# One visit instead of two: the products of scores and values behind the last chunk of a head pair

## The chip, the cores and the metric

The kernel runs on one core of a Trainium2 chip. The metric is the device time of one execution in microseconds (us); the median of three runs of the kernel before is 1099.41 us (1097.35 to 1099.85).

## The reference

One decoder layer on a sequence of 512 tokens with 2048 channels in float32. The normalised input is projected; one half of the result goes through a recurrent mixer with 16 heads of 64 channels, the other through a pooling group; both are gated, joined, projected back and added to the input, and a gated per-layer embedding and a last normalisation follow. What matters here is the recurrence of a head and the group normalisation behind it:

```python
    def step(S, inp):
        r_t, w_t, k_t, v_t, kk_t, a_t = inp
        sa = jnp.einsum('bhvk,bhk->bhv', S, -kk_t)
        S = (S * w_t[:, :, None, :]
             + sa[..., None] * (kk_t * a_t)[:, :, None, :]
             + v_t[..., None] * k_t[:, :, None, :])
        y_t = jnp.einsum('bhvk,bhk->bhv', S, r_t)
        return S, y_t
...
        y = wkv7_scan(rh, wh, kh, vh, kk, ah)
        y = head_group_norm(y, ln_w[i], ln_b[i])
```

## The kernel before, in words

**Chunks, hops and pairs.** The 16 heads are taken as 8 pairs (j, 128 channels each), and the 512 tokens as 8 chunks (ch) of 64 tokens. Within a chunk the recurrence is written with matrices, so that only the state goes from chunk to chunk. The function recur (from L756) does this for one pair. For each chunk it issues on TensorE:

- the output product (L784, py<-sbd,ar): the state (sbd) times the chunk's queries and keys. VectorE adds one half of it to mv (L787, zs);
- the solve product (L793, psu; pu in the profile), whose result ScalarE copies into uv (L797), the chunk's corrected values;
- the state product (L802, pss; ps in the profile), from which VectorE makes the next state (L809, sbd), and GpSimd the part s0p that the hop behind it adds (L816).

Each of these three steps hangs on the one before through VectorE or ScalarE. The way from one to the next is called a hop. So that TensorE does not wait, pump(n) puts n matmuls of other work behind each: 9 behind the state product (HC3), 6 behind the output product (HC1), 9 behind the solve product (HC2). This other work is one long stream: the large projections of coming pairs and of the pooling group (zk, zr, zv, zg, zb in the profile, 128x512 each, with weights and inputs split into a high and a low part, three matmuls per block) and at the end the embedding's (pple).

**The outputs.** The outputs of four chunks share one PSUM bank: a tile py of 128x512, one for chunks 0 to 3 and one for chunks 4 to 7. To the output products are added the products of scores (mt) and values (uv) within a chunk (L824): for each of four chunks and each of the two heads a 128x64 by 128x64 product into 64 of the bank's 128 partitions. TensorE is used there as two tiles of 64 columns, and an even chunk's and an odd chunk's product alternate. In the profile they are py<-uv,mt, 128*64; a visit is an unbroken run of them. One visit stands behind the state product of chunk 3, the other behind chunk 7's solve product, since the last chunk needs no new state. Behind each visit ScalarE copies the two halves of the bank into ysb (L830).

**Behind the hops.** From ysb VectorE makes statistics (L845, eight), aggregates (L847, eight), the inverse root (L850, then L143 to L151) and the normalised values (L854, eight). The function finish transposes them on TensorE (L861, pyt), and ScalarE and VectorE apply scale, bonus and gate.

**Between two pairs** the function gather (from L678) prepares the next one: on TensorE the decay and rate products (pu, pa), transposes of values (pv) and keys (pbk), the products pmv and the key norm's pss (L566), with pump between them; on ScalarE the tanh (L532, sig), the exponentials (L539 pw, L540 ipw) and copies (L690, L700 bkn, L712, L713); on VectorE the running sum of the log decay (L533, L534, sig).

**PSUM.** Four pools share the eight banks. The pool psY has two banks, and in turn they hold half of the score tiles (pm, in chunk 0), py of chunks 0 to 3, py of chunks 4 to 7 and pv of the next pair. The pool psM has three, for most other products, pbk, pmv and pss among them.

**What sets the order.** Matmuls are held in the order of the program (mm, L157 in the profile). On the other engines the framework's planner puts the instructions in order: by the program's order as priority, by its own estimate of when inputs are there, and with the hop's own steps (L787, L797, L809) far ahead by a high_priority. Each engine then works through its list in that order. The weights of the stream come by DMA from SyncE's queue; ScalarE rounds them (L132, whi) and VectorE takes the rest (L133, wlo).

## Time and profile before

| | |
|---|---|
| runs, us | 1099.85, 1097.35, 1099.41 |
| span of the profiled execution, us | 1095.9 |
| all py<-uv,mt records | 256, 16 visits of 16, 222 ns each (median) |
| ysb<-py copies on ScalarE | 32, 367 ns each |
| statistics st<-ysb on VectorE | 64, 214 ns each |
| aggregates mvr<-st on VectorE | 64, 152 ns each |

The profiled execution is one of its own; the table gives its span, from the first to the last instruction, and the times of the runs include what lies around it. The matmul records of this profile come two for each product of plain float32, which is done in two passes. Ends of matmuls are modelled and overlap; the distance from one start to the next is what a matmul costs in a stream. A row of the timeline has the start and length in us, the engine (PE is TensorE, PEld its weight loads, DVE VectorE, ACT ScalarE, POOL GpSimd), the line, the operation, output<-inputs, shapes and the count of merged records; in brackets stands the idle time before it and what ended it. A row of the waits has who waited, for whom, total us, times and longest.

### The profile page before, as it was taken

To read this page: it belongs to the slowest core of one execution; us is meant where nothing else is said; L and a number is where in the kernel's file an instruction comes from. 1 tells how busy PE (TensorE), PEld (TensorE's weight loads), DVE (VectorE), ACT (ScalarE), POOL (GpSimd) and SP (SyncE) were. 2 spreads that over 40 slices of the span, in tenths; PEclk is the share of its full clock that TensorE was granted. 3 is DMA by queue.
4 is the path that set the end of the run, shared out by engine and by line. 5 is a ranking of instruction groups with operands and counts; after the bars stand their busy time and mean duration, and the time that the engine had idled before them with its cause. 6 is when DMAs were issued, how large, how long until landed. Compare 5 with 4: busy or idle time off the path is not lost.

```text
span 1095.9 us, 17196 instructions
## 1 busy us (share of the span) xinstructions
PE 1070.8 (98%) x6060; PEld 877.6 (80%) x6060; DVE 708.2 (65%) x1835; ACT 448.3 (41%) x917; POOL 76.9 (7%) x180
## 2 busy tenths in 40 slices
PE   5999999999999999999999999999999999999996
PEld 4888878887788888788878788888888888888885
DVE  6687867878688679678886956454433424445366
ACT  7633535345335335353343344543222222233337
POOL 2100110110110110100101101000000000000000
PEclk9999999999999999999999999999999999999999
DMA  7433433332423333333334242775534438455534
GB/s 233 116 96 97 111 92 84 96 100 73 120 82 105 104 92 89 96 82 93 91 94 119 79 138 93 232 233 169 172 124 136 167 99 244 137 189 137 181 106 154
DMA packets 178486, 138.56 MB, mean 126 GB/s; under 512 B 34678, under 2 KB 139743, under 8 KB 178399
## 3 DMA queue, kind: packets, MB, share of 16 engines
q1 hardware_dynamic: 157694, 103.89, 32.1%
q10 hardware_dynamic: 20704, 33.56, 9.8%
q8 instruction: 48, 0.79, 0.3%
q14 instruction: 40, 0.32, 0.1%
HBM read 118.02 MB, written 18.87 MB: 125 GB/s over the span
## 4 chain that ended last, share of the span: by engine, by line
PE 86%; DVE 5%; DMA 4%; ACT 3%; issue 1%; SPq 0%; ACTq 0%; DVEq 0%
PE acc_o L157 16%; PE zb L157 14%; PE acc_g L157 14%; PE zv L157 8%; PE zk L157 7%; PE zg L157 7%; PE zr L157 7%; PE py L157 2%; PE pple L157 2%; PE pm L157 1%; PE pu L157 1%; DMA n<-nd 1%; PE pp L157 1%; DMA raw_g<-in_w_pg_dram 1%; PE ps L157 1%
## 5 line engine op out<-in xcount | busy, mean ns | idle before, releaser
L133 DVE TENSOR_TENSOR wlo_g<-raw_g,whi_g 128x512 fp32r<-128x512 f32 x84 | 57.0, 685 | 79.6 <-ACT whi_g L132 76.5
L157 PE MATMUL zb<-hhi,whi_b 128*128 128x512 f32 x256 | 107.0, 418 | 0.0
L133 DVE TENSOR_TENSOR wlo_o<-raw_o,whi_o 128x512 fp32r<-128x512 f32 x64 | 43.9, 690 | 91.4 <-ACT whi_o L132 91.4
L157 PE MATMUL zb<-hhi,wlo_b 128*128 128x512 f32 x256 | 100.5, 393 | 0.0
L157 PE MATMUL acc_o<-whi_o,ylo 128*128 128x512 f32 x256 | 100.2, 391 | 0.0
L157 PE MATMUL acc_o<-whi_o,yhi 128*128 128x512 f32 x256 | 99.9, 390 | 0.0
L157 PE MATMUL zb<-hlo,whi_b 128*128 128x512 f32 x256 | 99.9, 390 | 0.0
L157 PE MATMUL acc_o<-wlo_o,yhi 128*128 128x512 f32 x256 | 99.8, 390 | 0.0
L132 ACT CAST whi_g<-raw_g 128x512 fp32r<-128x512 f32 x84 | 51.9, 620 | 102.7 <-PE acc_g L157 55.4
L157 PE MATMUL acc_g<-whi_g,x2hi 128*128 128x512 f32 x208 | 81.3, 391 | 0.0
L157 PE MATMUL acc_g<-wlo_g,x2hi 128*128 128x512 f32 x208 | 80.9, 389 | 0.0
L157 PE MATMUL acc_g<-whi_g,x2lo 128*128 128x512 f32 x208 | 80.7, 389 | 0.0
L132 ACT CAST whi_o<-raw_o 128x512 fp32r<-128x512 f32 x64 | 39.9, 623 | 97.0 <-PE acc_o L157 96.7
L816 POOL TENSOR_SCALAR s0p<-sbd,pw 64x64 f32<-64x64 f32 x96 | 56.6, 589 | 322.8 <-DVE sbd L809 255.0
L132 ACT CAST whi_b<-raw_b 128x512 fp32r<-128x512 f32 x64 | 39.7, 621 | 86.5 <-PE zv L157 35.4
L133 DVE TENSOR_TENSOR wlo_b<-raw_b,whi_b 128x512 fp32r<-128x512 f32 x64 | 43.8, 685 | 34.2 <-ACT whi_b L132 32.9
L157 PEld LDWEIGHTS zb<-hhi,wlo_b 128*128 128x128 f32 x256 | 48.0, 188 | 11.1
L661 DVE TENSOR_TENSOR xw<-xw,tm 128x60 f32<-128x60 f32 (+24 forms) x248 | 52.1, 210 | 6.8
L157 PEld LDWEIGHTS acc_o<-wlo_o,yhi 128*128 128x128 f32 x256 | 48.1, 188 | 10.3 <-DVE wlo_o L133 0.4
L157 PEld LDWEIGHTS acc_o<-whi_o,yhi 128*128 128x128 f32 x256 | 48.1, 188 | 9.7
L157 PEld LDWEIGHTS acc_o<-whi_o,ylo 128*128 128x128 f32 x256 | 48.1, 188 | 9.8
L157 PEld LDWEIGHTS zb<-hhi,whi_b 128*128 128x128 f32 x256 | 48.2, 188 | 8.5
(285 smaller groups left out, 2550.0 us busy)
## 6 DMA issues: line engine op xcount, KB each, us to landing
raw_b<-in_w_in_dram SPq DMA_DIRECT2D x64, 256.0 KB
raw_o<-in_w_out_dram SPq DMA_DIRECT2D x64, 256.0 KB
raw_g<-in_w_pg_dram SPq DMA_DIRECT2D x64, 256.0 KB
raw_k<-in_w_in_dram SPq DMA_DIRECT2D x32, 256.0 KB
raw_r<-in_w_in_dram SPq DMA_DIRECT2D x32, 256.0 KB
raw_v<-in_w_in_dram SPq DMA_DIRECT2D x32, 256.0 KB
raw_g<-in_w_in_dram SPq DMA_DIRECT2D x32, 256.0 KB
n<-nd SPq DMA_DIRECT2D x16, 256.0 KB
```

The costliest lines, as they stand in the source:

```text
L132: nc.scalar.copy(hi, raw)
L133: nc.vector.tensor_tensor(lo, raw, hi.bitcast(F32), ALU.subtract)
L157: i = nc.tensor.matmul(*a, **k)
L661: nc.vector.tensor_tensor(xw[:, 0:n_, s + 1:32], xw[:, 0:n_, s + 1:32], tm[:, 0:n_, 0:w_], ALU.add)
L816: nc.gpsimd.tensor_scalar(s0p[hc, :], nxt[hc, hc], pcn[hc], None, ALU.mult)
```

## The change

The visit behind chunk 3 is taken out, and its eight products and two copies are put in front of those behind chunk 7. Both py tiles are kept in a dictionary until then. Order and number of the products, the copies and everything else of the program stay.

```diff
@@ -770,7 +770,7 @@
         ysb = rw.tile([P, NT, P], F32, name=f"ysb{j}", tag="t", bufs=4)
-        py = None
+        pys = {}
         for ch in range(NCH):
@@ -778,7 +778,8 @@
             if ch % 4 == 0:
-                py = psY.tile([P, T], F32, name=f"py{j}_{ch}", tag="y")
+                pys[ch // 4] = psY.tile([P, T], F32, name=f"py{j}_{ch}", tag="y")
+            py = pys[ch // 4]
             zs = zsp[par]
@@ -814,20 +815,21 @@
-            if ch % 4 == 3:
-                for qq in range(2):
-                    for h in range(2):
-                        for pr in range(2):
-                            c_ = ch - 3 + 2 * qq + pr
-                            yr = slice(64 * pr, 64 * pr + 64)
-                            o_ = (2 * qq + pr) * P + 64 * h
-                            mm(py[yr, o_:o_ + 64], mt[:, pr, 2 * (c_ // 2) + h, pr, :],
-                                             uv[:, c_, 64 * h:64 * h + 64], start=False, stop=True,
-                                             skip_group_check=True)
-                py4 = py.rearrange("p (s c) -> p s c", c=P)
-                for pr in range(2):
-                    yr = slice(64 * pr, 64 * pr + 64)
-                    nc.scalar.copy(ysb[yr, q - 1:q + 1, :], py4[yr, pr::2, :])
+            if ch == NCH - 1:
+                for c0 in range(0, NCH, 4):
+                    py = pys[c0 // 4]
+                    for qq in range(2):
+                        for h in range(2):
+                            for pr in range(2):
+                                c_ = c0 + 2 * qq + pr
+                                yr = slice(64 * pr, 64 * pr + 64)
+                                o_ = (2 * qq + pr) * P + 64 * h
+                                mm(py[yr, o_:o_ + 64], mt[:, pr, 2 * (c_ // 2) + h, pr, :],
+                                   uv[:, c_, 64 * h:64 * h + 64], start=False, stop=True, skip_group_check=True)
+                    py4 = py.rearrange("p (s c) -> p s c", c=P)
+                    for pr in range(2):
+                        yr = slice(64 * pr, 64 * pr + 64)
+                        nc.scalar.copy(ysb[yr, c0 // 2:c0 // 2 + 2, :], py4[yr, pr::2, :])
             step()
```

## The prediction

> **What bounds the kernel now.** I read the page first, then the waits of TensorE, then the timeline around the two places where the products of scores and values stand.

> ```profile
> span 1095.9 us, 17196 instructions
> PE 1070.8 (98%) x6060; PEld 877.6 (80%) x6060; DVE 708.2 (65%) x1835; ACT 448.3 (41%) x917; POOL 76.9 (7%) x180
> PE 86%; DVE 5%; DMA 4%; ACT 3%; issue 1%; SPq 0%; ACTq 0%; DVEq 0%
> 137.90:720.00 582.10, 578.60 (x3658) 470.94 (x3658) 442.17 (x1330) 245.79 (x535) 64.23 (x112) 1.00 0.37 104
> ```

> The last row is a stretch that holds all eight pairs' hops (its columns: length, then busy time of PE, PEld, DVE, ACT, POOL, then the granted clock, 1.00, and DMA). TensorE is busy 578.6 of 582.1 us there, so a change counts by what it does to TensorE's stream: work taken out of it, or a wait put into it. The waits in the same stretch (total, times, longest) are few:

> ```profile
> PE py L157 <- DVE sbd L809: 1.6, 4, 0.9
> PE pss L157 <- ACT bkn L700: 0.9, 2, 0.5
> PE pu L157 <- DVE zs L787: 0.4, 1, 0.4
> PEld py L157 <- DVE sbd L809: 5.2, 9, 1.4
> ```

> The profiled execution is known by its span, 1095.9 us; the median of the three runs, 1099.41, lies 3.5 us above it and includes what surrounds the program. I work out differences on the span and put them on the median. 0.2%, about what a measurement of this kernel can tell from no change, is 2.2 us.

> **The visit that goes (behind chunk 3).** Pair 0, TensorE, behind chunk 3 and then, for comparison, behind chunk 5, where no products stand:

> ```profile
> 155.36 0.38 PE L157 MATMUL ps<-uv,bkn 128*128 128x128 f32 x2
> 155.68 0.69 PE L157 MATMUL py<-uv,mt 128*64 128x64 f32 x16
> 156.29 0.50 PE L157 MATMUL zk<-hhi,whi_k 128*128 128x512 f32 x1
> 158.47 0.38 PE L157 MATMUL py<-sbd,ar 128*128 128x128 f32 x2
> ...
> 162.38 0.38 PE L157 MATMUL ps<-uv,bkn 128*128 128x128 f32 x2
> 162.52 0.47 PE L157 MATMUL zr<-hhi,whi_r 128*128 128x512 f32 x1
> 164.68 0.38 PE L157 MATMUL py<-sbd,ar 128*128 128x128 f32 x2
> ...
> 605.95 0.38 PE L157 MATMUL ps<-uv,bkn 128*128 128x128 f32 x2
> 609.06 0.38 PE L157 MATMUL py<-sbd,ar 128*128 128x128 f32 x2
> ```

> Between the state product and the next chunk's output product lie nine matmuls of the projection in both cases. With the visit that takes 158.47 - 155.36 = 3.11 us, without it 164.68 - 162.38 = 2.30. Pair 6, the last two rows, gives 3.11 again; the other pairs lie between. The visit costs 0.81 us, 8 x 0.81 = 6.5 us in all, and all of it lies on TensorE's path. (Eight products are sixteen records: each is done in two passes.)

> **The visit that grows (behind chunk 7).** The sixteen records reappear there, behind sixteen others. A visit with 32 small tiled records exists in the kernel already, pmv in the gathering step:

> ```profile
> 564.57 1.15 PE L157 MATMUL pmv<-uv,mt 64*64 64x64 f32 x32
> 565.65 0.50 PE L157 MATMUL pss<-kqh,blk 128*128 128x512 f32 x1
> 181.12 0.69 PE L157 MATMUL py<-uv,mt 128*64 128x64 f32 x16
> 208.26 2.06 PE L157 MATMUL pm<-ar,bk 64*128 64x128 f32 x32
> ```

> 32 records take 1.15 us where 16 take 0.69: 16 more cost 0.46 us. The next large matmul starts 565.65 - 564.57 = 1.08 after the visit's first record, against 156.29 - 155.68 = 0.61 for 16, which is 0.47. So the streaming part moves and the rest, 0.81 - 0.47 = 0.34 us, vanishes: getting into and out of the products is paid once per pair and not twice. New is that the merged visit goes from one PSUM bank to another in its middle. The scores (pm, last row) change the bank at every product and run 32 records of twice the columns in 2.06 us, about twice 1.15 less the fixed part, so I take 0 for the change of bank; the upper end is a whole visit's fixed 0.34 us, at which nothing would be gained. 8 x 0.34 gives **-2.7 us**.

> **The cover that chunk 3's hop loses.** Its state product now has 2.30 us until the next output product, as at the other hops. The wait of that output product is VectorE's sbd. The tightest case behind chunk 3 is one of the pairs where a weight split stands between the two updates:

> ```profile
> 306.73 0.29 DVE L809 SCALAR_TENSOR_TENSOR sbd<-ps,pw,s0p 64x64 f32<-64x64 f32 x1
> 308.44 0.38 PE L157 MATMUL py<-sbd,ar 128*128 128x128 f32 x2
> ```

> The update ends at 307.02, 1.42 us before its reader. 0.81 less leaves 0.61 us, so I put the lost cover at nothing; what it costs if VectorE comes late is the second rival.

> **The copies, and what is queued behind them.** ScalarE's two copies of the first four chunks and VectorE's four statistics and four aggregates leave the hop of chunk 3, where nobody on TensorE waited for them, and join the others behind chunk 7. Pair 0 there:

> ```profile
> 181.88 0.74 ACT L830 COPY ysb<-py 64x256 f32<-64x256 f32 x2 [0.27 <-PE py L157]
> 184.36 0.30 ACT L524 CAST us<-ur 128x128 fp32r<-128x128 f32 x1 [1.73 <-PE pu L157]
> 187.58 0.63 ACT L539 ACTIVATE pw<-sig 128x512 f32<-128x512 f32 x1 [0.57 <-DVE rs L151]
> 189.27 1.07 ACT L700 COPY bkn<-pbk 128x512 f32<-128x512 f32 x2
> 182.66 0.61 DVE L845 BATCH_NORM_STATS2 st<-ysb 128x6 f32<-128x64 f32 x4 [0.32 <-ACT ysb L830]
> 183.18 0.37 DVE L847 BATCH_NORM_AGGREGATE mvr<-st 128x2 f32<-128x6 f32 x4
> 183.58 0.17 DVE L850 TENSOR_SCALAR ve<-mvr 128x8 f32<-128x8 f32 x1
> 186.26 1.22 DVE L534 TENSOR_TENSOR_SCAN sig<-seg,sig 128x512 f32<-128x512 f32 x1
> 189.64 0.75 DVE L854 TENSOR_SCALAR ysb<-ysb,mvr,rs 128x64 f32<-128x64 f32 x3
> 184.84 0.60 PE L161 MATMUL pv<-ident,sv 128*128 128x128 f32 x4
> 189.90 0.50 PE L157 MATMUL pss<-kqh,blk 128*128 128x512 f32 x1 [0.45 <-ACT bkn L700]
> 193.22 0.60 PE L161 MATMUL pyt<-ident,ysb 128*128 128x128 f32 x4
> ```

> ScalarE is idle 1.73 us behind its copies, so 0.74 us more of them fits, and what is queued behind them (the casts of us and then sig) still finds its input late. The first bank is now held until the end of the pair, and the transposes pv want one of the two banks of its pool; the first two copies end about 1.5 us behind the visit's start, the transposes come 184.84 - 181.12 = 3.7 us behind it: no wait. VectorE's chain gets later: the last copy ends 0.74 later, so four of the statistics start at about 2.3 us behind the visit's start; four statistics (0.52 from the first to what follows) and the aggregates (0.1 each with what follows, two of them in the gap ahead of the last copy) put L850 at about 3.4 where it stands 183.58 - 181.12 = 2.46 now. That is 0.9 later, or 0.44 against TensorE, whose own stream is 0.46 later there. For the normalised outputs that is covered: L854 ends at 190.39, its reader pyt stands at 193.22. The tightest is the last pair, where 712.67 - 711.79 = 0.88 us are left for the 0.44:

> ```profile
> 711.03 0.76 DVE L854 TENSOR_SCALAR ysb<-ysb,mvr,rs 128x64 f32<-128x64 f32 x3
> 712.67 0.60 PE L161 MATMUL pyt<-ident,ysb 128*128 128x128 f32 x4
> ```

> Nothing that moves issues a DMA or stands in the queues of SyncE and GpSimd.

> The place with no slack is the other wait of the list above: VectorE's scan (L534) shares its queue with this chain, ScalarE's pw waits for the scan, the bkn copies stand behind pw, and TensorE's pss waits 0.45 us for a bank that a bkn copy frees. The scan is threaded between the steps of the chain as soon as its input is there, so with the chain shifted it can take a place one or two steps earlier and start when it starts now. I take 0, with bounds of -0.9 (both listed waits of pss vanish) and +0.44 in each of the three pairs (0, 2 and 4) where pw stands ahead of bkn, +1.3 us.

> [...] By the rows, the copy reads 181.88 - 181.81 = 0.07 us behind the end of 16 records, and behind 32 records it is no later:

> ```profile
> 565.76 0.26 ACT L712 COPY zs<-pmv 64x128 f32<-64x128 f32 x1 [1.16 <-PE pmv L157]
> ```

> Those 32 end at 564.57 + 1.15 = 565.72, 0.04 us before the copy of an idle ScalarE. [...]

> The sum is -2.7 us: 1099.4 - 2.7 = **1096.7 us**.

> **The rivals.**

> Pss waits longer (no measurable change). If the scan keeps its place in VectorE's order, three gathers lose 0.44 us: -2.7 + 1.3 = -1.4, or 1098.0. For it speaks that the order is written by a planner that has its own idea of the durations; against it, that in pairs 1, 3 and 5 the bkn copies already stand ahead of pw. [...] I give it 2 in 100, as the row above shows no tail.

> The planner turns pw and bkn round (more gain). With the scan planned later, the bkn copies are ready first and pss waits for nothing, as in pairs 1, 3 and 5: -2.7 - 0.9 = -3.6, or 1095.8.

> The hop of chunk 3 loses its cover (slower). The mechanism: in the stretch that shrinks from 3.11 to 2.30 us, a weight split (0.69 us) or two stand ahead of the state update on VectorE, as at nine other places now, where the weight load waits 5.2 us in all. With the longest wait that TensorE shows there, 0.9 us, in each pair, the time is -2.7 + 8 x 0.9 = +4.5, or 1103.9. It eats the gain from 0.34 us per pair on and is slower by over 0.2% from 0.34 + 0.28 = 0.62 on. Against it: 0.61 us of slack are left at the tightest pair, and the statistics leave that very stretch.

> The change does not do what it says: the matmuls keep the order of the program, so the visits do merge; that only a move within an idle stretch results is excluded by 578.6 of 582.1.

> **How the numbers follow.** The sum as it stands 50 in 100, more gain 12, longer waits of pss 26 (the tail among them), merged visit with a price at the change of bank 4, the lost cover 8. The likeliest case by itself spans 1096.2 to 1097.3, half a microsecond for waits that fall elsewhere in a new order. The range goes from the case with more gain, with 1 us of spread of the runs below it, 1094.8, to the longer waits of pss with 1.4 above, 1099.4. Faster by over 0.2% (below 1097.2) are the case with more gain and nine tenths of the likeliest: 0.57. Within 0.2%: the rest of the likeliest, the pss case and the bank: 0.35. Slower: 0.08.

> **What would show it.** Right: one visit of 32 py records per pair, about 1.15 us long, with the next large matmul about 1.08 behind its start; 2.30 us from state product to output product behind chunk 3; the sum of the hops shorter by 0.34 us per pair. Wrong: a gap inside the 32 records, waits of py for sbd behind chunk 3, or waits of pss for bkn above 0.9 us in all.

## The result and the profile after

The changed kernel takes 1105.41 us (median of six runs, 1102.93 to 1110.24) where the kernel before, run beside it, takes 1099.56 (six runs, 1097.35 to 1100.93). The ratio is 1.0061, with a 95% interval of 1.0043 to 1.0080: it is slower by 5.9 us, where 2.7 us less were predicted. In the experiments further down, one of the eleven runs of the kernel before with its preparation held back took 2747 us, for no cause that the record shows, and the ratios leave it out.

The page of the changed kernel opens with its span and the engines' busy time:

```profile
span 1103.6 us, 17200 instructions
PE 1072.4 (97%) x6060; PEld 878.1 (80%) x6060; DVE 708.0 (64%) x1835; ACT 449.6 (41%) x917; POOL 76.4 (7%) x180
```

The span is 7.7 us longer than before, TensorE's busy time 1.6 us, so most of the loss is waiting (the visits alone should have made that busy time shorter; a stretch at half clock, below, makes it longer). The waits of TensorE in the changed kernel (who, for whom, total us, times, longest) name the places:

```profile
PE py L157 <- DVE sbd L810: 2.8, 4, 1.0
PE pyt L161 <- DVE ysb L856: 2.8, 4, 1.3
PE pq L157 <- DVE y L734: 2.4, 2, 1.6
...
PE pss L157 <- ACT bkn L700: 0.7, 2, 0.4
```

The waits of pyt (the transposes of the normalised outputs, in finish) and of pq (what hangs on VectorE's L734, in the same step) were not in the list before. The four transposes of a group wait one by one for their pieces, and most of that is put down to their weight loads:

```profile
PEld pyt L161 <- DVE ysb L856: 5.0, 14, 0.8
```
TensorE's timeline in pair 0 shows that the visits themselves did what was predicted, first chunk 3, then chunk 7:

```profile
156.16 0.38 PE L157 MATMUL ps<-uv,bkn 128*128 128x128 f32 x2
...
158.46 0.38 PE L157 MATMUL py<-sbd,ar 128*128 128x128 f32 x2
181.11 1.15 PE L157 MATMUL py<-uv,mt 128*64 128x64 f32 x32
182.19 0.50 PE L157 MATMUL zv<-hhi,whi_v 128*128 128x512 f32 x1
```

From state product to output product behind chunk 3 it is 158.46 - 156.16 = 2.30 us; the 32 records take 1.15 us without a gap, and the next large matmul starts 1.08 us behind the first. Taking every matmul of the two profiles in order and comparing when it starts, the eight visits behind chunk 3 give 0.80 us each and the eight behind chunk 7 cost 0.47 each: -2.6 us. The same comparison gives the loss: +6.6 at pyt, +2.5 at pq, +0.9 at py for sbd, +1.6 in a stretch at half clock. That is +9.0, of the 9.6 us by which the stretch of the pairs gets longer. Behind the pairs 1.6 us come off: from the last transpose on, the profiled execution of before takes 382.7 us, the changed kernel 381.1, and so do most other kernels here, so that part says nothing about the change.

**Where pyt waits.** A word on the pairs first: in the gathering step behind pair 1, the products pv, pbk and pmv are pair 2's, but pu, pss and VectorE's preparation (kp, ar, bk and what they need) are already pair 3's; the same holds behind every pair. "The preparation" and "the prepared pair" mean that one here. VectorE's timeline in this step, before:

```profile
258.11 0.17 DVE L850 TENSOR_SCALAR ve<-mvr 128x8 f32<-128x8 f32 x1
258.32 0.17 DVE L143 TENSOR_SCALAR rs<-ve 128x8 int32<-128x8 int32 x1
...
263.40 0.16 DVE L151 SCALAR_TENSOR_TENSOR rs<-nt,rs 128x8 f32<-128x8 f32 x1
263.48 0.42 DVE L593 TENSOR_SCALAR tha<-tha 128x512 f32<-128x512 f32 x1
263.81 1.88 DVE L854 TENSOR_SCALAR ysb<-ysb,mvr,rs 128x64 f32<-128x64 f32 x8
```

And after:

```profile
260.10 0.17 DVE L852 TENSOR_SCALAR ve<-mvr 128x8 f32<-128x8 f32 x1
260.20 0.69 DVE L133 TENSOR_TENSOR wlo_b<-raw_b,whi_b 128x512 fp32r<-128x512 f32 x1
260.81 0.17 DVE L143 TENSOR_SCALAR rs<-ve 128x8 int32<-128x8 int32 x1
...
264.88 0.69 DVE L594 TENSOR_TENSOR ar<-sr,pw 128x512 f32<-128x512 f32 x1
265.48 0.16 DVE L151 SCALAR_TENSOR_TENSOR rs<-nt,rs 128x8 f32<-128x8 f32 x1
265.56 0.68 DVE L596 TENSOR_TENSOR bk<-kp,ipw 128x512 f32<-128x512 f32 x1
266.16 0.16 DVE L149 TENSOR_TENSOR nt<-rs,ve 128x8 f32<-128x8 f32 x1
266.24 0.75 DVE L597 SCALAR_TENSOR_TENSOR ar<-sk,dprm,pw 128x512 f32<-128x512 f32 x1
266.90 0.16 DVE L150 TENSOR_TENSOR nt<-nt,rs 128x8 f32<-128x8 f32 x1
266.98 0.69 DVE L568 TENSOR_SCALAR kk<-pss 128x512 f32<-128x512 f32 x1
...
268.35 1.82 DVE L856 TENSOR_SCALAR ysb<-ysb,mvr,rs 128x64 f32<-128x64 f32 x8
```

The chain of the normalised outputs (ve, eleven small steps of the inverse root, eight normalised pieces) takes 263.81 + 1.88 - 258.11 = 7.6 us before and 268.35 + 1.82 - 260.10 = 10.1 after. No step of it got slower: more of the preparation (L594, L596, L597) and of other work that is ready (L568, L734, a weight split L133) stands between its steps, 0.4 to 0.75 us each. Before, such work stood between the steps too, but fewer pieces of it. To compare kernels I set each time against the start of the step's first large product (pu<-uhh,us), and take the transposes with it. Before and after on TensorE:

```profile
258.46 0.39 PE L157 MATMUL pu<-uhh,us 128*128 128x512 f32 x1
267.49 0.60 PE L161 MATMUL pyt<-ident,ysb 128*128 128x128 f32 x4
```

```profile
259.52 0.39 PE L157 MATMUL pu<-uhh,us 128*128 128x512 f32 x1
268.98 1.57 PE L161 MATMUL pyt<-ident,ysb 128*128 128x128 f32 x4 [0.26 <-DVE ysb L856]
```

Before, the chain starts 0.35 us ahead of pu, ends 7.23 behind it, and pyt starts at 9.03. After, it starts 0.58 behind pu, ends at 10.65, and the four transposes take 1.57 us instead of 0.60, each waiting for its piece. So a start that is 0.92 us later became an end that is 3.4 later.

**Why the start is 0.92 later and not the predicted 0.44.** Of the two lists of answers about kql (the low part of the prepared pair's split keys), before and after, these lines give its first and last start:

```profile
L138 DVE TENSOR_TENSOR kql<-kk,kqh x6: 684/686/693, 167.3 to 538.4; 128x512 fp32r<-128x512 f32 x6
```

```profile
L138 DVE TENSOR_TENSOR kql<-kk,kqh x6: 654/656/658, 183.4 to 565.5; 128x512 fp32r<-128x512 f32 x6
```

The split moved from chunk 5, at 167.3, to behind chunk 7, at 183.4. Nothing in the change touches it, but kqh (the high part, made by ScalarE), kql and ysb are handed out of the same four buffers (tag t) in the program's order, and ysb's first writer, the copy that was behind chunk 3, now stands behind chunk 7. ScalarE's timeline in pair 1 of the changed kernel shows kqh between the copies, and VectorE's shows kql in the middle of statistics and aggregates:

```profile
256.98 0.74 ACT L832 COPY ysb<-py 64x256 f32<-64x256 f32 x2 [0.93 <-PE py L157]
257.75 0.62 ACT L137 CAST kqh<-kk 128x512 fp32r<-128x512 f32 x1
258.40 0.75 ACT L832 COPY ysb<-py 64x256 f32<-64x256 f32 x2
```

**The clock.** Behind pair 2's pyt, TensorE's timeline of the changed kernel, and the window behind it (length, busy time of PE, PEld, DVE, ACT, POOL, granted clock, DMA share, GB/s):

```profile
344.21 0.39 PE L157 MATMUL zb<-hhi,wlo_b 128*128 128x512 f32 x1
345.90 1.57 PE L161 MATMUL pyt<-ident,ysb 128*128 128x128 f32 x4 [1.30 <-DVE ysb L856]
347.23 0.48 PE L157 MATMUL zb<-hhi,whi_b 128*128 128x512 f32 x1
...
347.87 0.63 PE L157 MATMUL zb<-hhi,wlo_b 128*128 128x512 f32 x1
348.30 0.63 PE L157 MATMUL zb<-hhi,whi_b 128*128 128x512 f32 x1
```

```profile
347.70:351.00 3.30, 3.30 (x10) 2.52 (x9) 3.30 (x3) 1.20 (x2) 0.00 (x0) 0.50 0.04 13
```

After 347.23 - 344.21 = 3.02 us from one large matmul to the next, the clock falls to 0.50, and the large matmuls stand 0.43 us apart instead of 0.23; the trace's record has the half clock for 3.413 us from 347.64 on. The stretch of the same length before it, 344.23 to 347.64, was not idle: it held the end of one large matmul, the four transposes and the first 0.4 us of the next large ones, with 1.83 us of TensorE's busy time in it. The longer runs of the changed kernel have the lower mean clock: 1102.93 us at 0.998, 1110.24 at 0.994.

### The profile page after: what moved, and what is told of

Its sections match the earlier page's. It is cut to its first block, busy times and chain, and to the rows that moved or that the text cites. A ratio compares the mean times of both kernels' runs of the same rounds, so it can differ in the third digit from the quotient of the medians.

```text
span 1103.6 us, 17200 instructions
## 1 busy us (share of the span) xinstructions
PE 1072.4 (97%) x6060; PEld 878.1 (80%) x6060; DVE 708.0 (64%) x1835; ACT 449.6 (41%) x917; POOL 76.4 (7%) x180
## 5 line engine op out<-in xcount | busy, mean ns | idle before, releaser
L133 DVE TENSOR_TENSOR wlo_g<-raw_g,whi_g 128x512 fp32r<-128x512 f32 x84 | 56.8, 683 | 81.9 <-ACT whi_g L132 81.8
L157 PE MATMUL zb<-hhi,whi_b 128*128 128x512 f32 x256 | 107.5, 420 | 0.0
L133 DVE TENSOR_TENSOR wlo_o<-raw_o,whi_o 128x512 fp32r<-128x512 f32 x64 | 43.9, 690 | 92.3 <-ACT whi_o L132 92.3
L157 PE MATMUL zb<-hhi,wlo_b 128*128 128x512 f32 x256 | 101.3, 396 | 0.0
L157 PE MATMUL zb<-hlo,whi_b 128*128 128x512 f32 x256 | 100.5, 393 | 0.0
L157 PE MATMUL acc_o<-whi_o,ylo 128*128 128x512 f32 x256 | 100.2, 391 | 0.0
L157 PE MATMUL acc_o<-whi_o,yhi 128*128 128x512 f32 x256 | 99.9, 390 | 0.0
L157 PE MATMUL acc_o<-wlo_o,yhi 128*128 128x512 f32 x256 | 99.7, 389 | 0.0
L157 PE MATMUL acc_g<-whi_g,x2hi 128*128 128x512 f32 x208 | 81.2, 391 | 0.0
L157 PE MATMUL acc_g<-wlo_g,x2hi 128*128 128x512 f32 x208 | 80.9, 389 | 0.0
L157 PE MATMUL acc_g<-whi_g,x2lo 128*128 128x512 f32 x208 | 80.7, 389 | 0.0
L133 DVE TENSOR_TENSOR wlo_b<-raw_b,whi_b 128x512 fp32r<-128x512 f32 x64 | 43.9, 688 | 34.7 <-ACT whi_b L132 33.3
L157 PEld LDWEIGHTS zb<-hhi,wlo_b 128*128 128x128 f32 x256 | 48.4, 189 | 11.2
L157 PEld LDWEIGHTS acc_o<-wlo_o,yhi 128*128 128x128 f32 x256 | 48.1, 188 | 10.0
L157 PEld LDWEIGHTS acc_o<-whi_o,yhi 128*128 128x128 f32 x256 | 48.1, 188 | 9.7
L157 PEld LDWEIGHTS zb<-hhi,whi_b 128*128 128x128 f32 x256 | 48.9, 191 | 8.6
L157 PEld LDWEIGHTS acc_o<-whi_o,ylo 128*128 128x128 f32 x256 | 48.1, 188 | 9.7
```

What stands on the lines that cost most here:

```text
L133: nc.vector.tensor_tensor(lo, raw, hi.bitcast(F32), ALU.subtract)
L157: i = nc.tensor.matmul(*a, **k)
```

## The experiments

The theory from the two traces: the chain of the normalised outputs starts later (by the copies and statistics, and by the split keys), VectorE's planned order then puts more of the preparation between its steps, it ends behind its reader, and TensorE waits at pyt. Rivals: the merged visit itself costs something; only the buffer order matters; it is a matter of a sum of small delays, not of a cover that is used up. Ratios are against the kernel before, run on the same chip. It takes 1098.06 us beside the first four kernels below, 1096.54 beside the two with one small delay, the control with the preparation held back and the kernel claimed and held, and 1097.57 beside the other four. L-numbers shift by a few lines between kernels.

**Only the copies late, with two visits.** The products stay where they were; the four copies stand behind chunk 7, the second bank's first:

```diff
+            if ch == NCH - 1:
+                for c0 in (4, 0):
+                    py4 = pys[c0 // 4].rearrange("p (s c) -> p s c", c=P)
+                    with tc.issue_after(uvc.ins):
+                        for pr in range(2):
+                            yr = slice(64 * pr, 64 * pr + 64)
+                            uvc = nc.scalar.copy(ysb[yr, c0 // 2:c0 // 2 + 2, :], py4[yr, pr::2, :])
```

> The products stand in two visits as in the kernel before; only the copies to ysb, and with them the statistics, come late: all four copies stand behind chunk 7's visit, the second bank's first. If lateness of the normalisation is the cause, the waits of pyt come although no visit was merged, and the visits' 2.7 us are not gained: 1104 to 1109 us, waits of TensorE for ysb and y of 4 us or more. If the merged visit or the bank that it holds is the cause, the time is that of the kernel before, 1099.6 within 1 us.

Measured: 1123.67 us (1118.58 to 1123.99), ratio 1.0221 (1.0197 to 1.0245), far above the 1104 to 1109 expected. Its waits, and one of its stretches at half clock:

```profile
PE pyt L161 <- DVE ysb L857: 11.8, 5, 4.3
```

```profile
275.00:281.80 6.80, 4.97 (x13) 3.50 (x14) 6.68 (x15) 1.39 (x2) 0.00 (x0) 0.50 0.00 0
```

The slowdown needs no merged visit. The buffers move here as in the changed kernel, since ysb's first writer is late here too (kql starts at 184.7 in pair 0). The chain starts 2.03 us later than before here and ends 7.4 later (pair 1, by the timeline as above); the wait of 4.3 us leaves 6 us between large matmuls and is followed by 6.83 us at half clock.

**Only the statistics late.** The kernel before; the copies stay behind chunk 3, and the four statistics of its chunks are queued behind the other four:

```diff
-        for i in range(8):
-            nc.vector.bn_stats(st[:, i, :], y8[:, i, :])
+        for i in range(4, 8):
+            last = nc.vector.bn_stats(st[:, i, :], y8[:, i, :])
+        with tc.issue_after(last.ins):
+            for i in range(4):
+                nc.vector.bn_stats(st[:, i, :], y8[:, i, :])
```

> The kernel before, with products and copies where they were; only the four statistics of the first four chunks are queued on VectorE behind the other four. If some 0.9 us more of VectorE's work behind chunk 7 are enough to thread the preparation of the pair after next between the steps of the inverse root, pyt waits for ysb here as well: 1101 to 1105 us. If the cause is the buffer (ysb is first written at chunk 7, so that the split of the key's squares, kqh and kql, which shares its buffers, is pushed behind chunk 7), nothing happens here, because the copies stay: 1099.6 within 1 us.

Measured: 1108.82 us (1106.72 to 1111.85), ratio 1.0101 (1.0079 to 1.0122). The side was right, the size was not: 10.8 us, more than the 5.9 of the change and more than the 8.5 that it loses before the visits' gain of 2.6 is taken off. Its waits are those of the changed kernel, almost number for number:

```profile
PE py L157 <- DVE sbd L809: 3.1, 4, 1.9
PE pyt L161 <- DVE ysb L857: 2.7, 4, 1.2
PE pq L157 <- DVE y L734: 2.4, 2, 1.6
```

Neither the merged visit nor the other buffer order is in this kernel (kql starts at 167.8 in pair 0, as before). VectorE's lateness alone is enough.

**The buffer claimed early.** The changed kernel with one small write by GpSimd to ysb behind chunk 3, so that the buffers go round as before:

```diff
+            if ch == 3:
+                nc.gpsimd.memset(ysb[:, 0, 0:1], 0.0)
```

> The changed kernel, and GpSimd clears one column of ysb at chunk 3, so that its buffer is taken at chunk 3 as in the kernel before. If the pushed split of the key's squares (0.62 us on ScalarE, 0.66 on VectorE) is the cause, the waits of pyt go and the visits' gain shows: 1096 to 1098 us. If the lateness of the statistics alone is enough, a good part of the waits stays: 1099 to 1104 us.

Measured: 1095.84 us (1093.16 to 1099.63), ratio 0.9985 (0.9972 to 0.9999): a little faster than before, at the edge of what the interval can tell. No wait of pyt or pq is left in its list, and kql starts at 166.5 in pair 0, where it stood before the change. The chain starts 0.53 us later than before, against the 0.44 predicted, so the other 0.39 us of the changed kernel were the split keys, ScalarE's half and VectorE's together.

**The preparation held back.** The changed kernel, with VectorE's part of the preparation queued behind the last normalised piece of the pair that ends:

```diff
-            prepare(j + 1)
+            if done[0] is None:
+                prepare(j + 1)
+            else:
+                with tc.issue_after(done[0].ins):
+                    prepare(j + 1)
```

> The changed kernel, and VectorE's preparation of the pair after next (kp, ar, bk and what follows) is queued behind the last normalised value instead of between the steps of the inverse root. If it is this threading that makes ysb late, the waits of pyt go: 1095.5 to 1098.5 us, 2.6 below the kernel before as the visits are. If ysb is late because the chain starts late, the waits stay at half or more: 1101 us or above.

Measured: 1097.01 us (1094.93 to 1098.17), ratio 0.9984 (0.9973 to 0.9996). VectorE's timeline, pair 1, and the waits:

```profile
258.66 0.17 DVE L852 TENSOR_SCALAR ve<-mvr 128x8 f32<-128x8 f32 x1
...
263.38 1.88 DVE L856 TENSOR_SCALAR ysb<-ysb,mvr,rs 128x64 f32<-128x64 f32 x8
```

```profile
PE pm L157 <- DVE bk L600: 2.0, 2, 1.4
```

The chain starts as late as in the changed kernel (0.57 behind pu at 258.09) and takes 6.6 us instead of 10.1. So the threaded preparation is what made it long. The preparation is late in its turn, and a new wait of the score products pm for bk gives 2.0 us back.

**The preparation held back, kernel before.** The same edit as a control:

> The kernel before with VectorE's part of the next preparation queued behind the last normalised output. Control for the runs that hold it: if the merged visit is worth what TensorE's records say (2.6 us) this kernel stays at 1097.5 to 1099.5, 1 to 3 above the changed kernel with the same order; if the order alone made that kernel faster than the one before, it comes to 1095.5 to 1097.

Measured: 1097.41 us, ratio 1.0004 (0.9995 to 1.0014). Without a chain that is late, holding the preparation brings nothing, so the 2.2 us between the two ratios go with the visit.

**Half of the statistics late; the split keys late.** Two kernels, each the kernel before with one small delay: statistics 2 and 3 queued behind the others, or VectorE's half of the split, kql, queued behind the pair's last aggregate (ScalarE's half, kqh, stays where it was, first at 166.3; in the changed kernel it moved too):

```diff
+        for i in (0, 1, 4, 5, 6, 7):
+            last = nc.vector.bn_stats(st[:, i, :], y8[:, i, :])
+        with tc.issue_after(last.ins):
+            for i in (2, 3):
+                nc.vector.bn_stats(st[:, i, :], y8[:, i, :])
```

```diff
-        split(kqh, kql, kk)
+        if done[0] is None:
+            split(kqh, kql, kk)
+        else:
+            with tc.issue_after(done[0].ins):
+                split(kqh, kql, kk)
```

> The kernel before with its two visits, only two of the four statistics of the first four chunks queued behind those of the last four. Two statistics and what stands behind them are some 0.3 to 0.45 us, half of what the four brought. Theory of lateness with a threshold (the chain of the normalised outputs is threaded with the next preparation once it is more than about 0.55 to 0.75 us later): hardly any wait of the transposes pyt, 1098 to 1100. If the cost grows in step with the lateness instead: about half of the 10.8 us that four statistics cost, 1102 to 1105. If lateness is not the cause and only the buffer order counts: as before, 1098.

> The kernel before with its two visits and its copies and statistics in place, only the split of the scaled keys of the next pair (kqh on ScalarE, kql on VectorE, 0.62 and 0.66 us) queued behind the last aggregate of the pair. Theory that the buffers' order alone makes the slowdown: 1103 to 1106 with waits of pyt for the normalised outputs, as in the changed kernel. Theory that the lateness of the copies and statistics makes it: 1097 to 1100, the 0.66 us of kql covered by what the chain has left against pyt.

Measured: half the statistics 1097.67 us, ratio 1.0015 (1.0006 to 1.0024); the split keys 1097.81 us, ratio 1.0009 (1.0000 to 1.0018). The chain starts 0.39 and 0.46 us later, and the wait of pyt in their lists is, in turn:

```profile
PE pyt L161 <- DVE ysb L857: 0.7, 1, 0.7
```

```profile
PE pyt L161 <- DVE ysb L858: 1.1, 2, 0.7
```

Half of the four statistics cost 1.6 us, the four 11. A split that comes late on VectorE is by itself not the cause either, though it makes the chain later than the buffers did in the changed kernel (0.46 against 0.39). What kqh costs where it stands between ScalarE's copies was not tried alone.

**Both small delays together.** To tell a sum from a cover that is used up:

> The kernel before with its two visits, with both of the delays that by themselves cost 1.6 us (two statistics late, chain 0.39 us later) and 1.0 us (split of the next keys late, chain 0.46 us later). Theory that the chain of the normalised outputs costs little below a lateness of about 0.6 us and much above it: chain 0.85 us later, waits of pyt in most pairs, 1104 to 1109 on a chip where the kernel before takes 1097 to 1098. Rival that the costs just add: 1099 to 1101.

Measured: 1104.72 us (1103.75 to 1105.29), ratio 1.0062 (1.0049 to 1.0075): 6.8 us, where 1.6 and 1.0 add to 2.6. Its wait of pyt:

```profile
PE pyt L161 <- DVE ysb L861: 2.9, 5, 0.7
```

That is most of the 8.5 us that the change loses before its gain, made in the kernel before out of two delays that cost little one by one. The mean clock of its five runs is 0.997 to 0.998, as that of the kernel before beside it, so the half clock isn't needed for a loss of this size.

**The reader moved.** The changed kernel with the transposes pyt behind 13 more projection matmuls of the gathering step:

```diff
-        pump(H5)
+        pump(H5 + HX)
         if pending:
             pending.pop()()
-        pump(HX)
```

> The changed kernel with only the reader moved: the transposes pyt stand 13 projection matmuls (some 3 us of TensorE) later in the next gathering step; VectorE's chain stays as late as in the changed kernel. If the loss is TensorE waiting for the chain at pyt, and the half clock behind such a wait: both vanish, 1095 to 1098. If VectorE's threading costs TensorE elsewhere too (pq, sbd): 1098 to 1102. If the merged visit itself costs: 1103 to 1106 as the changed kernel.

Measured: 1094.20 us (1092.22 to 1094.70), ratio 0.9964 (0.9952 to 0.9977), below the range expected, the fastest kernel of the study and 3.4 us below the median of before beside it. VectorE and TensorE in pair 1:

```profile
267.45 1.83 DVE L855 TENSOR_SCALAR ysb<-ysb,mvr,rs 128x64 f32<-128x64 f32 x8
```

```profile
258.63 0.39 PE L157 MATMUL pu<-uhh,us 128*128 128x512 f32 x1
271.06 0.60 PE L161 MATMUL pyt<-ident,ysb 128*128 128x128 f32 x4
```

The chain is as long and as late as in the changed kernel, 10.65 us behind pu. Only its reader stands at 12.43 instead of 9.46, and the loss is gone.

**The reader moved, kernel before.** The control:

> The kernel before with the transposes pyt moved in the same way, as the control. They wait for nothing there, so no gain is expected: 1096.5 to 1099, and 1 to 3 above the changed kernel with the same move if the merged visit is worth its 2.6 us.

Measured: 1098.57 us, ratio 1.0009 (1.0000 to 1.0018). Where nothing waits at pyt the move gains nothing.

**Two remedies at once.** The changed kernel with the early claim and either the preparation held back or the reader moved:

> The changed kernel with both remedies: the output buffer claimed at chunk 3 and VectorE's part of the next preparation queued behind the last normalised output. If both remedies remove the same cost: 1095.5 to 1097, as either alone. If they add: 1093.5 to 1095.5. If holding the preparation makes its own late pieces the next wait (pm for bk): 1096.5 to 1098.5.

> The changed kernel with the output buffer claimed at chunk 3 and pyt moved 13 matmuls later. No wait of pyt is left to remove once the buffer is claimed, so as the early claim alone, 1095 to 1097; under 1094.5 only if the move also gives VectorE back something at sbd.

Measured: 1095.03 us, ratio 0.9988 (0.9979 to 0.9997), and 1095.78 us, ratio 0.9986 (0.9976 to 0.9996): about as the early claim or the held preparation alone (0.9985, 0.9984), so they do not add. (The first time by itself lies where adding was expected, but the kernel before is 1.5 us faster beside it than beside the single remedies; the ratio takes that out.) The reader moved alone stands at 0.9964, and claiming the buffer as well took some of that back; the intervals touch, and the cause stays open. In the first, the waits have moved to the hops:

```profile
PE py L157 <- DVE sbd L810: 4.6, 5, 1.7
```

All kernels in one table, by the chain's start: pair 1's chain (start of ve, end of the last normalised piece) and start of pyt, in us behind the step's first product, then the stretch from the first output product to the last transpose, and the ratio.

| kernel | ve | end | pyt | stretch | ratio |
|---|---|---|---|---|---|
| before | -0.35 | 7.23 | 9.03 | 575.1 | |
| before, preparation held | -0.35 | 6.25 | 9.03 | 575.6 | 1.0004 |
| before, reader moved | -0.35 | 7.22 | 12.43 | 575.7 | 1.0009 |
| half the statistics late | 0.04 | 9.04 | 9.03 | 575.1 | 1.0015 |
| split keys late (kql alone) | 0.11 | 9.71 | 9.03 | 578.1 | 1.0009 |
| after, claimed early | 0.18 | 8.23 | 9.03 | 574.3 | 0.9985 |
| after, claimed, held | 0.18 | 6.79 | 9.03 | 576.9 | 0.9988 |
| after, claimed, reader moved | 0.18 | 8.23 | 12.43 | 573.6 | 0.9986 |
| four statistics late | 0.42 | 10.65 | 9.46 | 585.2 | 1.0101 |
| both small delays | 0.50 | 10.65 | 9.46 | 583.6 | 1.0062 |
| after | 0.57 | 10.64 | 9.45 | 584.7 | 1.0061 |
| after, preparation held | 0.57 | 7.16 | 9.03 | 574.0 | 0.9984 |
| after, reader moved | 0.57 | 10.65 | 12.43 | 573.2 | 0.9964 |
| two visits, late copies | 1.68 | 14.64 | 13.46 | 598.7 | 1.0221 |

A kernel is slow where the end stands well behind 9.03 and the reader isn't moved, whatever made it late and whether it has one visit or two. A start that is 0.4 to 0.5 us later makes the end 1.0 to 2.5 later, one that is 0.8 to 0.9 later 3.4. In this pair the cover of 1.8 us is used up at about 0.4. Other pairs have another cover, 1.04 to 2.85 us where a preparation goes on: with one small delay one to three of them wait at pyt, with both or with the change all six. Behind the last two pairs nothing is left to prepare; there the chain takes 5.01 and 4.91 us in the changed kernel, 5.95 and 5.55 before, and pyt waits for nothing.

## Why the prediction was wrong, point by point

**The visits: right.** 0.80 us saved behind chunk 3 and 0.47 paid behind chunk 7, where 0.81 and 0.47 stood, no price for the change of bank. The first bank's copies start 0.05 us behind its sixteenth record. The second bank's stand behind the first's or behind kqh, and with the buffer claimed early they start 0.40 us behind the visit's end without ScalarE having waited, so a copy's delay behind 32 records was at most that here. The forecast's 2 in 100 is for a tail that grows with the records, copies that start later the more records stand ahead of them: no run shows one, and in the kernel before the copy starts 0.07 us behind 16 records and 0.04 behind 32. The gain shows where nothing eats it: with the reader moved in both, the stretch is 573.2 against 575.7 us (-2.5), with the preparation held in both 574.0 against 575.6 (-1.6, with pm's new wait in it). By the ratios it is 0.9964 against 1.0009 and 0.9984 against 1.0004, so 4.9 and 2.2 us; why the first is more than the 2.6 of the records stays open.

**The failed step: "For the normalised outputs that is covered: L854 ends at 190.39, its reader pyt stands at 193.22."** The cover of 2.83 us in pair 0 was read rightly, and so was the lateness by copies and statistics (0.44 predicted, 0.53 with the buffer claimed early). What failed is that the lateness was carried unchanged from the chain's start to its end. The prediction saw that the scan "is threaded between the steps of the chain" and asked only what that does for the scan. Each operation that gets in between is paid by the chain: in pair 0 its end moved from 6.47 to 9.61 us behind pu, 3.14 for a start that is 0.92 later, and the reader at 9.30 waited. The last pair, which the prediction called the tightest, has no preparation behind it and lost nothing. Holding the preparation back, with the same late start, takes the whole loss away.

**What was left out: the buffers.** The prediction moved the copies in the queues, not in the order of the shared buffers. By that order the prepared pair's split keys moved from chunk 5 to behind chunk 7 and made the other half of the lateness, 0.39 of 0.92 us. Claiming the buffer early takes it back and with it the loss; the delay of VectorE's half by itself costs 1.0 us, so it was the two together. That the buffers' order moves the split is shown by the early claim; why the planner puts the preparation between the chain's steps, and not behind them, was not tried.

**The rivals.** The slower rival put the loss at the hop of chunk 3. That hop takes 2.30 us in all eight pairs, so its cover held. The waits of py for sbd did grow from 1.6 to 2.8 us, but behind chunk 2, and what matched matmuls show of it is 0.9 us in all, a tenth of the loss. Pss waits 0.7 us instead of 0.9, so "I take 0" held for the scan. The chance of 0.08 for slower was too small: pyt, the reader at which most of the lateness then showed, had been closed with one subtraction, and pq, the other one, isn't in the prediction.

## What to carry to other kernels

Before you call a late chain covered, look at what shares its engine: where a planner can put other work between its steps, a late start of 0.9 us became a late end of 3.4, so compare the reader's place with the chain's end as it would be with that work in it. When a write moves, list what is handed out of the same buffers behind it, since that moves too, with no line of the diff naming it. If a change gains on the engine that bounds the kernel and makes a reader wait, try the reader's place first: 13 matmuls later turned a loss of 5.9 us into a gain of 3.4.

## What the runs showed of the hardware

The place may count too. In the kernel with late copies the half clocks start at 196.50, 275.00 and 435.43 us, 78.50 and 160.43 apart, which is 23.0 and 47.0 times the 3.413 that the changed kernel's record has for the one behind pyt. In the changed kernel the half clock at the end of the span, from 1098.58 us on, starts 750.93 behind that one, 220.0 times 3.413. So in both traces they start on a grid of that step. The gap of 3.10 us (193.11 to 196.21) lies within one step of it, 193.09 to 196.50; the gap of 3.09 (512.69 to 515.78) is cut by the grid at 513.93, and the clock stays full:

```profile
196.50:199.91 3.41, 3.41 (x9) 2.64 (x8) 3.41 (x3) 1.39 (x2) 0.00 (x0) 0.50 0.08 24
513.93:517.35 3.42, 2.61 (x11) 1.81 (x12) 3.42 (x11) 0.90 (x2) 0.00 (x0) 1.00 0.30 81
```

Where other work than transposes filled the gap, 3.76 us (the changed kernel with the preparation held back, 506.50 to 510.26, with a wait of 1.39 and 32 score products) brought no half clock either (mean clock 0.998, as before); whether by its place or its filling isn't shown. That the place decides is my estimate from the gaps of 3.10 and 3.09; the changed kernel's gap of 3.02, from 344.21 on, begins 0.02 us ahead of a step, 344.23. The half clock cost the changed kernel 1.6 us on top of the wait of 1.3 us ahead of it.

Two PSUM banks in one visit cost nothing that could be seen: the 32 records run in 1.15 us, as the 32 of pmv do in one bank.
